# z in products of 512 columns, with its Silu placed anew and the background steps paced anew

## The chip, the cores and the metric

The kernel runs on one core of one Trainium2 chip. The metric is the device time of one execution in microseconds, as the median over runs.

## The reference

One decoder layer on 256 tokens of width 1024, in float32: a SwiGLU block, then a mixer with two branches side by side (a Mamba-2 branch, "ssd", and differential attention), then a second SwiGLU block, each with an RMS norm before and after it. The mixer multiplies its normed input `u` by one wide matrix and cuts the result in pieces:

```python
z, xbc, dt_raw, q, k, v, gate_logits = jnp.split(u @ w_in[l], IN_SPLITS, axis=-1)
...
y = y.reshape(b, L, SSD_D_INNER) * jax.nn.silu(z)
y = rmsnorm(y.reshape(b, L, SSD_GROUPS, SSD_D_INNER // SSD_GROUPS), 1.0).reshape(b, L, SSD_D_INNER) * norm_g
return y @ w_branch
...
gates = jax.nn.sigmoid(gate_logits + gate_b[l]).reshape(b, L, N_BRANCH, D_MODEL)
merged = gates[:, :, 0] * y_ssd + gates[:, :, 1] * y_att
```

z has 2048 columns. Its Silu gates the output of the ssd branch before that branch's group norm.

## The kernel before

**Products in split precision.** Each float32 operand is split in a high part and a low remainder that TensorE takes as float32r: a cast on ScalarE gives the high part (`whi`, L250), a subtraction on VectorE the low one (`wlo`, L253). A product is then the sum of three: high by high, high by low and low by high. `u` is kept with its high and low parts side by side (`[..., 0, :]` and `[..., 1, :]`), 256 tokens each.

**Two forms of such a product.** Both take a chunk of 1024 x 256 weights, as two halves of 128 output columns, with eight k-tiles each.
- `mm_t` (L294) writes 256 columns of one accumulator per half: per k-tile one product of `whi` with the high part of `u` (L301), one of `whi` with its low part (L302), and one of `wlo` with its high part (L304). One accumulator bank holds both halves, and one copy evicts it.
- `mm_w` (L306) multiplies `whi` with both parts of `u` at once, 512 columns (L316), and `wlo` with the high part, 256 columns (L315, L318). Each half has a bank of its own; the eviction is a copy of its second 256 columns on ScalarE (L320, or L323 with a scale) and an add of the first 256 on VectorE (L321, or L324).

Both take their accumulators from `pj`, three banks of PSUM; the other five are `bg`, for everything in the background.

**The order of the mixer.** Products of `u`: v, dt, B and C, then xs (eight chunks with `mm_w`), z (eight chunks with `mm_t`), q and k (four chunks each, with `mm_w`), the gates (L1375, `pgt`), then the ssd branch's output product (`pws`), the attention's (`pwd`) and the layer's. The last ones use `natural`, which takes half a token block at a time ("a call" below: 12 products of 512 columns).

**The background.** Between chunks `back.run(us)` hands out steps of generators in a queue. Each step yields a cost in microseconds written by hand; `run` adds its argument to a balance and takes steps until the balance is used up. A step that yields `BREAK` ends the run at hand and leaves the balance. The generators, in the order of the queue:
- `ssd_work`, per group of heads: two steps `X` (transposes `px`, L1061, and a product, 0.6 each), four steps `E` (1.4 each: small Relu and Exp on ScalarE, a clamp and a product with `cbm` on VectorE, from `acb`, which POOL's queue loads) and one with the products `py` (L1093, 1.6). They need the table with Exp.
- `ssd_norm`, per group, two under way at a time: 1.2 (the product with Silu(z), L1107, and a square), 1.5, a `BREAK`, 0.1 (the sum `pn`, L1119, and Ln and Exp) and 2.8 (the split to `yh`, `yl`).
- `att_work`: scores `psc` (L1166, L1167), softmax (2.3 a head), the turn `pa` (L1201), the combination (1.3 a head), `BREAK`, values `po` and a norm (1.8), the turn `pto` (L1240, 0.8), over pairs of heads.

The arguments are the constants `BG_US` (z), `QK_US` (q and k), `GATE_US` (gates) and `SSD_US` (`pws`, and the first half of `pwd`). `take()` hands out a chunk's weights and splits those three chunks ahead; the loads on SP's queue follow the splits.

**Who sets the order.** From the ends of the feed-forward blocks on, the planner of the framework orders each engine's instructions from their dependencies and their order in the code. After `own_order(PE)` (L1351), from the gates on, TensorE keeps the order of the code. `act_table(name)` loads a table of functions on ScalarE and ties itself behind all earlier `act()` calls and ahead of all later ones, so no Exp runs between the load of the Silu table (L1333) and the next load (L1336). Plain copies and casts aren't tied.

Of the kernel before, what the change touches and what calls it, by code (L numbers as in the profile page):

```python
# [18 lines left out]
AF = mybir.ActivationFunctionType  # L19
# [4 lines left out]
EXP_LN = "natural_log_exp_and_others"  # L24
# [3 lines left out]
T = 256  # L28
# [12 lines left out]
WARM = 3  # L41
FILL = 2
TAIL = 3
BG_US = 3.15
QK_US = 2.4
GATE_US = 1.75
SSD_US = 1.55
DOWN = {"f1": "p q1 p p q2 p ppp", "f2": "q1 p q2 p q3 ppp"}
FIRST, LAST = (1, 2, 3, 5, 7, 6, 4), (1, 6, 7, 2, 5, 3, 4)
BREAK, STOP = object(), object()  # L50
# [3 lines left out]
def tile_hybrid_layer(ctx: ExitStack, tc: tile.TileContext, x, ffn1_pre_g, ffn1_w_gate, ffn1_w_up,  # L54
# [4 lines left out]
    nc = tc.nc  # L59
# [5 lines left out]
    def k4(shape, name, dt=F32):  # L65
        return sb.tile(shape, dt, tag="k4", name=name, bufs=K4_BUFS)
# [4 lines left out]
    def k2(shape, name, dt=F32):  # L71
        return sb.tile(shape, dt, tag="k2", name=name, bufs=K2_BUFS)
# [7 lines left out]
    def pj(name):  # L80

        return ps.tile([P, 512], F32, tag="pj", name=name, bufs=3)

    def pjt(name):

        return pj(name).rearrange("p (m t) -> p m t", m=2)

    def bg(shape, name):
        return ps.tile(shape, F32, tag="bg", name=name, bufs=5)
# [169 lines left out]
    def split_to(n):  # L259

        while len(splits) < min(n, len(units)):
            of, p = units[len(splits)]
            if p is not None:
                splits.append(of.split(p))
                continue
            for _ in split_steps():
                pass

    def ahead_of(i, n):

        n *= 4
        while n > 0 and i < len(units):
            n -= 4 if units[i][1] is None else 1
            i += 1
        return i

    def take(ahead=AHEAD):

        i = taken[0]
        taken[0] += 1  # L280
        split_to(ahead_of(i, ahead))
        (of, p), w = units[i], splits[i]
        splits[i] = None
        if p is not None:
            return w
        his, los = w
        nj = chunks[of][1][1] // 2
        return (lambda j: his[j // nj][:, j % nj, :], lambda j: los[j // nj][:, j % nj, :])
# [5 lines left out]
    def mm_t(acc, w, act, k0=0, first=True, last=True, ks=range(KD)):  # L294

        (wh, wl), (ah, al, _) = w, act
        acc = acc if isinstance(acc, list) else [acc[:, m, :] for m in range(2)]
        for m in range(2):
            cs = slice(m * P, (m + 1) * P)
            for j in ks:  # L300
                nc.tensor.matmul(acc[m], wh(j)[:, cs], ah(k0 + j), start=first and j == ks[0], stop=False)  # L301
                nc.tensor.matmul(acc[m], wh(j)[:, cs], al(k0 + j), start=False, stop=False)  # L302
            for j in ks:
                nc.tensor.matmul(acc[m], wl(j)[:, cs], ah(k0 + j), start=False, stop=last and j == ks[-1])  # L304

    def mm_w(dst, name, w, act, scale=None):  # L306


        (wh, wl), (ah, _, ahl) = w, act
        for m in range(2):  # L310
            acc = pj(f"{name}{m}")
            cs = slice(m * P, (m + 1) * P)
            for j in range(KD):
                if j:
                    nc.tensor.matmul(acc[:, :T], wl(j)[:, cs], ah(j), start=False, stop=False)  # L315
                nc.tensor.matmul(acc, wh(j)[:, cs], ahl(j), start=j == 0, stop=j == KD - 1)  # L316
                if not j:
                    nc.tensor.matmul(acc[:, :T], wl(j)[:, cs], ah(j), start=False, stop=False)  # L318
            if scale is None:
                nc.scalar.copy(dst[:, m, :], acc[:, T:])  # L320
                nc.vector.tensor_tensor(dst[:, m, :], acc[:, :T], dst[:, m, :], ALU.add)  # L321
            else:
                nc.scalar.activation(dst[:, m, :], acc[:, T:], AF.Copy, scale=scale)  # L323
                nc.vector.scalar_tensor_tensor(dst[:, m, :], acc[:, :T], scale, dst[:, m, :], ALU.mult, ALU.add)  # L324

    def mm_nat(acc, w, act, k0, first, last, late):
# [25 lines left out]
    order = mybir.DependencyInfo(mybir.DependencyClass.NoSync, mybir.DependencyReason.DATA)  # L352

    def act_table(name):
        f = nc.scalar.preload_act_table_set(name)
        for prev in act_since:
            tc.add_manual_dep(f.ins, prev, order, reason="activation table")
        act_since.clear()
        act_fence[0] = f.ins.name

    def act(*args, **kw):
        a = nc.scalar.activation(*args, **kw)
        if act_fence[0] is not None:
            tc.add_manual_dep(a.ins, act_fence[0], order, reason="activation table")
        act_since.append(a.ins.name)
# [65 lines left out]
    def new_u(tag):  # L431
        for i in range(2):
            uT[i] = sb.tile([P, 4, 2, T], F32R, tag="u8", name=f"u{i}_{tag}", bufs=2)

    act_u = (lambda j: uT[j // 4][:, j % 4, 0, :], lambda j: uT[j // 4][:, j % 4, 1, :],
             lambda j: uT[j // 4][:, j % 4, :, :])
# [594 lines left out]
    for i in range(4):  # L1031
        acc = k2([P, 2, T], f"bc{i}")
        mm_w(acc, f"pbc{i}", take(), act_u)
        dst = (bT, cT)[i // 2]
        conv(acc, 16 + 2 * i, dst[:, (i % 2) * 2:(i % 2) * 2 + 2, :])
        if i == 1:
            cumulated()
# [13 lines left out]
    sz = [None] * 4  # L1051
# [52 lines left out]
    def ssd_norm(groups):  # L1104

        def one(g):
            nc.vector.tensor_tensor(xs[g], xs[g], sz[g], ALU.mult)  # L1107
            sq = k4([P, 4, T], f"sqy{g}")
            nc.scalar.activation(sq, xs[g], AF.Square)
            yield 1.2  # L1110
            nc.vector.tensor_tensor(sq[:, 0:2, :], sq[:, 0:2, :], sq[:, 2:4, :], ALU.add)
            nc.vector.tensor_tensor(sq[:, 0, :], sq[:, 0, :], sq[:, 1, :], ALU.add)
            ssum = k2([P, 2, T], f"ssum{g}", F32R)
            split(ssum[:, 0, :], ssum[:, 1, :], sq[:, 0, :])
            yield 1.5
            yield BREAK
            pn = bg([P, T], f"pn{g}")
            for i in range(2):
                nc.tensor.matmul(pn, ones_r, ssum[:, i, :], start=i == 0, stop=i == 1)  # L1119
            rs = sq[:, 1, :]  # L1120
            act(rs, pn, AF.Ln, scale=1.0 / 512, bias=eps_c)
            act(rs, rs, AF.Exp, scale=-0.5)
            yield 0.1
            for c in range(4):
                n = col["ng"] + g * 4 + c
                nc.vector.scalar_tensor_tensor(xs[g][:, c, :], xs[g][:, c, :], cols_a[:, n:n + 1], rs,
                                               ALU.mult, ALU.mult)
            yh[g] = k4([P, 4, T], f"yh{g}", F32R)
            yl[g] = k4([P, 4, T], f"yl{g}", F32R)
            split(yh[g], yl[g], xs[g])  # L1130
            xs[g] = sz[g] = None
            yield 2.8

        todo = [one(g) for g in groups]
        under_way = []
        while todo or under_way:
            if todo and len(under_way) < 2:
                under_way.append(todo.pop(0))
            for w in list(under_way):
                us = next(w, None)  # L1140
                if us is None:
                    under_way.remove(w)
                else:
                    yield us
# [170 lines left out]
    back = Background()  # L1315
    back.add(cb_work())
    for g in range(4):
        xs[g] = k4([P, 4, T], f"xs{g}")
        for i in range(2):
            acc = k2([P, 2, T], f"xr{g}{i}")  # L1320
# [5 lines left out]
    for g in range(4):  # L1326
        sz[g] = k4([P, 4, T], f"sz{g}")
        for i in range(2):
            acc = pjt(f"pz{g}{i}")
            mm_t(acc, take(), act_u)  # L1330
            nc.scalar.copy(sz[g][:, i * 2:i * 2 + 2, :], acc)
            back.run(BG_US)
    act_table(SILU)  # L1333
    for g in range(4):
        act(sz[g], sz[g], AF.Silu)
    act_table(EXP_LN)  # L1336
    back.add(ssd_norm(range(4)))
    for c in range(4):
        if c % 2 == 0:
            qT[c // 2] = k4([P, 4, T], f"q{c}")  # L1340
            kT[c // 2] = k4([P, 4, T], f"k{c}")
        o = (c % 2) * 2
        mm_w(qT[c // 2][:, o:o + 2, :], f"pq{c}", take(), act_u, 0.125)
        back.run(QK_US)
        mm_w(kT[c // 2][:, o:o + 2, :], f"pk{c}", take(), act_u)
        back.run(QK_US)

# [41 lines left out]
    for q in range(2):  # L1389
# [3 lines left out]

        natural(f"pws{q}", 4, lambda j: yh[j // 4][:, j % 4, :], lambda j: yl[j // 4][:, j % 4, :], gated, SSD_US)
    yh = yl = None
# [18 lines left out]
    for q in range(2):  # L1414
# [4 lines left out]
        def merge(b, acc):  # L1419
# [5 lines left out]
        natural(f"pwd{q}", 2, lambda j: oh[j // 4][:, j % 4, :], lambda j: ol[j // 4][:, j % 4, :], merge,  # L1425
                SSD_US if q == 0 else 0.0, (attended, lambda: turn_merged(2))[q])

    pg = load_gain(mix_post_g, "pg_mx")
    acc = [[bg([P, 512], f"acc_mx{b}{q}") for q in range(2)] for b in range(2)]
# [47 lines left out]
```

## Time and profile before

| what | value |
|---|---|
| median of 3 runs | 737.26 us (736.78 to 737.35) |
| profiled execution | 735.83 us |
| its span | 734.1 us |
| granted TensorE clock | 0.998 |
| TensorE busy | 724.9 us (99%) |
| VectorE busy | 598.8 us (82%) |
| ScalarE busy | 469.3 us (64%) |
| z products | 287.5 to 342.2 us of the span |
| q and k products | 342.2 to 394.3 us |

The span is what the trace covers; the execution is 1.7 us longer than it. Engines are PE (TensorE's matmuls), PEld (its weight loads), DVE (VectorE), ACT (ScalarE), POOL (GpSimd) and SP (SyncE). L316 is line 316 of the kernel, and `out<-in` are the kernel's names for the tiles.

### The profile page before, as it was taken

Reading aid. Unit: us, or ns where it says so; the run is one execution under the profiler, and the core shown is the slowest. Engines: PE = TensorE matmul, PEld = TensorE weight load, DVE = VectorE, ACT = ScalarE, POOL = GpSimd, SP = SyncE. Lnnn points to the kernel's source line nnn. Section 1 sums busy time; section 2 is a strip of 40 time slices with the busy share of each in tenths; the row PEclk is TensorE's granted clock in tenths of the full one; section 3 lists DMA queues with packets and bytes.
Section 4 is the critical chain, followed back from the end, with each engine's and each line's share of the span. In section 5 each row is a group of like instructions: output and inputs, shape, how many; then the busy total and the mean of one; then the engine's idle time right before and its main releaser. Section 6 shows DMA issues by size and latency. Waiting matters only on the chain.

```text
span 734.1 us, 10526 instructions
## 1 busy us (share of the span) xinstructions
PE 724.9 (99%) x4019; PEld 618.1 (84%) x4019; DVE 598.8 (82%) x928; ACT 469.3 (64%) x801; POOL 39.4 (5%) x72
## 2 busy tenths in 40 slices
PE   8999999999999999999999999999999999999996
PEld 7888888888878889999888788888888888888884
DVE  6978767998679999777996997784774878779994
ACT  6656556665567676869965577772663657566562
POOL 2800000000300000000000000000020000000000
PEclk9999999999999999999999999999999999999999
DMA  8874774369453657656564664374471764664541
GB/s 293 236 251 153 226 231 173 138 212 363 125 172 118 189 156 240 211 170 212 154 224 147 208 215 148 138 250 181 134 233 35 230 204 155 215 223 142 188 164 57
DMA packets 94210, 137.92 MB, mean 188 GB/s; under 512 B 2684, under 2 KB 68304, under 8 KB 94160
## 3 DMA queue, kind: packets, MB, share of 16 engines
q1 hardware_dynamic: 91488, 129.51, 53.8%
q0 software_dynamic: 2368, 7.22, 3.0%
q8 instruction: 31, 0.51, 0.3%
q10 hardware_dynamic: 304, 0.53, 0.2%
q14 instruction: 19, 0.16, 0.1%
HBM read 136.17 MB, written 1.08 MB: 187 GB/s over the span
## 4 chain that ended last, share of the span: by engine, by line
PE 97%; DVE 1%; issue 1%; DMA 1%; ACT 0%; DVEq 0%; SPq 0%
PE pup_f L316 9%; PE pg_f L316 9%; PE pgt L335 6%; PE pws L335 6%; PE acc_f1p L625 5%; PE acc_f2p L625 4%; PE pxs L316 4%; PE pg_f L315 4%; PE pup_f L315 4%; PE pn_f L345 3%; PE pn_f L335 3%; PE pn_mx L335 3%; PE acc_mx L573 3%; PE pwd L335 3%; PE acc_f1p L573 3%; PE pz L301 2%
## 5 line engine op out<-in xcount | busy, mean ns | idle before, releaser
L253 DVE TENSOR_TENSOR wlo<-raw,whi 128x1024 fp32r<-128x1024 f32 (+1 forms) x226 | 267.1, 1210 | 23.1 <-ACT whi L250 21.9
L250 ACT CAST whi<-raw 128x1024 fp32r<-128x1024 f32 (+1 forms) x225 | 226.8, 1045 | 18.0 <-DMA raw<-in_ffn_w_down_dram 4.2
L316 PE MATMUL pup_f<-u_f,whi 128*128 128x512 f32 x288 | 101.3, 396 | 0.0
L316 PE MATMUL pg_f<-u_f,whi 128*128 128x512 f32 x288 | 101.2, 396 | 0.0
L315 PE MATMUL pg_f<-u_f,wlo 128*128 128x256 f32 x252 | 70.6, 280 | 0.0
L315 PE MATMUL pup_f<-u_f,wlo 128*128 128x256 f32 x252 | 70.3, 279 | 0.0
L316 PEld LDWEIGHTS pup_f<-u_f,whi 128*128 128x128 f32 x288 | 52.8, 188 | 9.8
L316 PEld LDWEIGHTS pg_f<-u_f,whi 128*128 128x128 f32 x288 | 52.8, 188 | 9.7
L315 PEld LDWEIGHTS pg_f<-u_f,wlo 128*128 128x128 f32 x252 | 47.5, 188 | 1.8
L315 PEld LDWEIGHTS pup_f<-u_f,wlo 128*128 128x128 f32 x252 | 47.5, 189 | 1.6
L316 PE MATMUL pxs<-u_mx,whi 128*128 128x512 f32 x128 | 44.6, 397 | 0.0
L321 DVE TENSOR_TENSOR su_f<-pup_f,su_f 128x256 f32<-128x256 f32 x36 | 15.2, 422 | 26.1 <-ACT su_f L320 25.9
L320 ACT COPY su_f<-pup_f 128x256 f32<-128x256 f32 x36 | 13.4, 371 | 35.3 <-PE pup_f L316 35.2
L130 ACT CAST wqh<-wt 128x1024 fp32r<-128x1024 f32 x20 | 21.1, 1053 | 23.0 <-DVE wt L122 17.9
L335 PE MATMUL pgt<-whi,u_mx 128*128 128x512 f32 x128 | 33.1, 393 | 0.0
L301 PE MATMUL pz<-u_mx,whi 128*128 128x256 f32 x128 | 31.8, 285 | 0.0
L302 PE MATMUL pz<-u_mx,whi 128*128 128x256 f32 x128 | 31.4, 283 | 0.0
L315 PE MATMUL pxs<-u_mx,wlo 128*128 128x256 f32 x112 | 31.2, 279 | 0.0
L335 PEld LDWEIGHTS pgt<-whi,u_mx 128*128 128x128 f32 x128 | 23.6, 188 | 5.4 <-issue 0.7
L316 PEld LDWEIGHTS pxs<-u_mx,whi 128*128 128x128 f32 x128 | 23.2, 188 | 4.2
L291 ACT CAST gh_f<-sg_f 128x512 fp32r<-128x512 f32 x18 | 11.2, 621 | 21.6 <-DVE sg_f L771 21.6
L301 PEld LDWEIGHTS pz<-u_mx,whi 128*128 128x128 f32 x128 | 24.5, 191 | 0.2 <-issue 0.2
(401 smaller groups left out, 1679.7 us busy)
## 6 DMA issues: line engine op xcount, KB each, us to landing
raw<-in_w_in_dram SPq DMA_DIRECT2D x40, 1024.0 KB, 5.4
raw<-in_ffn_w_down_dram SPq DMA_DIRECT2D x22, 1024.0 KB, 4.9
raw<-in_ffn_w_gate_dram SPq DMA_DIRECT2D x20, 1024.0 KB, 5.8
raw<-in_ffn_w_up_dram SPq DMA_DIRECT2D x20, 1024.0 KB, 5.5
raw<-in_ssd_w_branch_dram SPq DMA_DIRECT2D x8, 1024.0 KB, 5.0
acb<-acd POOLq DMA_DIRECT2D x8, 512.0 KB, 5.3
raw<-in_da_w_branch_dram SPq DMA_DIRECT2D x4, 1024.0 KB, 5.1
raw<-in_w_out_dram SPq DMA_DIRECT2D x4, 1024.0 KB, 5.6
```

What stands on the lines that cost most here:

```text
L130: nc.scalar.copy(hi, src)
L250: copy(hi[:, js, :], r[:, q * nj + j:q * nj + j + n, :])
L253: nc.vector.tensor_sub(lo[:, js, :], r[:, q * nj + j:q * nj + j + n, :], hi[:, js, :].bitcast(F32))
L301: nc.tensor.matmul(acc[m], wh(j)[:, cs], ah(k0 + j), start=first and j == ks[0], stop=False)
L302: nc.tensor.matmul(acc[m], wh(j)[:, cs], al(k0 + j), start=False, stop=False)
L315: nc.tensor.matmul(acc[:, :T], wl(j)[:, cs], ah(j), start=False, stop=False)
L316: nc.tensor.matmul(acc, wh(j)[:, cs], ahl(j), start=j == 0, stop=j == KD - 1)
L321: nc.vector.tensor_tensor(dst[:, m, :], acc[:, :T], dst[:, m, :], ALU.add)
L335: nc.tensor.matmul(acc, a(k0 + j), b(j), start=first and i == 0, stop=last and i == 11)
L345: nc.tensor.matmul(accs[b], x_(k0 + j), w_(j), start=first and j == 0 and w_ is wh and x_ is acts[b][0], stop=last and j == 3 and w_ is wl)
L573: nc.tensor.matmul(acc[b][q], x_[:, ts], w_(kt)[:, halves[q]], start=begin and i == 0 and kt == 0 and x_ is ah and w_ is wh, stop=i == n - ...
L625: nc.tensor.matmul(bank[p], x_, w_, start=p not in begun, stop=last and p in (1, 5, 6, 7))
```

## The change

Four things change.
- z is made by `mm_w` like xs, q and k; each half's copy and add write `sz[g]` directly.
- The last background run of the z stage goes. The Silu of groups 0 and 1 comes right behind z's last chunk. The Silu of groups 2 and 3, the load of the Exp table, the queueing of `ssd_norm` and a run of `BG_US` follow q's first chunk; `mm_w` remembers its last scaled copy, and those two Silus are tied behind it on ScalarE.
- `BG_US` 3.15 to 2.7, `QK_US` 2.4 to 2.6, `SSD_US` 1.55 to 1.75.
- `act()` takes the instruction to be tied behind as an argument.

```diff
-BG_US = 3.15
-QK_US = 2.4
+BG_US = 2.7
+QK_US = 2.6
 GATE_US = 1.75
-SSD_US = 1.55
+SSD_US = 1.75
...
-                nc.scalar.activation(dst[:, m, :], acc[:, T:], AF.Copy, scale=scale)
+                last_copy[0] = nc.scalar.activation(dst[:, m, :], acc[:, T:], AF.Copy, scale=scale).ins
...
-    def act(*args, **kw):
+    def act(*args, behind=None, **kw):
         a = nc.scalar.activation(*args, **kw)
+        if behind is not None:
+            tc.add_manual_dep(a.ins, behind.name, order, reason="behind a copy")
...
     for g in range(4):
         sz[g] = k4([P, 4, T], f"sz{g}")
         for i in range(2):
-            acc = pjt(f"pz{g}{i}")
-            mm_t(acc, take(), act_u)
-            nc.scalar.copy(sz[g][:, i * 2:i * 2 + 2, :], acc)
-            back.run(BG_US)
+            mm_w(sz[g][:, i * 2:i * 2 + 2, :], f"pz{g}{i}", take(), act_u)
+            if (g, i) != (3, 1):
+                back.run(BG_US)
     act_table(SILU)
-    for g in range(4):
+    for g in (0, 1):
         act(sz[g], sz[g], AF.Silu)
-    act_table(EXP_LN)
-    back.add(ssd_norm(range(4)))
     for c in range(4):
...
         mm_w(qT[c // 2][:, o:o + 2, :], f"pq{c}", take(), act_u, 0.125)
+        if c == 0:
+
+            for g in (2, 3):
+                act(sz[g], sz[g], AF.Silu, behind=last_copy[0])
+            act_table(EXP_LN)
+            back.add(ssd_norm(range(4)))
+            back.run(BG_US)
         back.run(QK_US)
```

More of the change, by code (lines that the diff above doesn't have):

```diff
@@ L304, in mm_t @@
                 nc.tensor.matmul(acc[m], wl(j)[:, cs], ah(k0 + j), start=False, stop=last and j == ks[-1])
+    last_copy = [None]
     def mm_w(dst, name, w, act, scale=None):
```

## The prediction

> **What bounds the kernel now.** I read the page first (span and the chain that ended last), then the chain in order of time, then the groups of single tiles, the busy time by stretches, and the order in time on each engine around the z products.
>
> ```profile
> span 734.1 us, 10526 instructions
> ...
> PE 97%; DVE 1%; issue 1%; DMA 1%; ACT 0%; DVEq 0%; SPq 0%
> ```
>
> The chain of work that ended last is 97% TensorE. So a cover lost elsewhere costs only once it reaches TensorE, and a product made cheaper is worth its whole saving. What a product costs is not its duration, which overlaps the next one's, but the step from one start to the next. The chain in order of time gives it (start, length, what):
>
> ```profile
> 34.86 0.46 PE pg_f L316 x2
> ...
> 129.96 0.47 PE pup_f L316 x2
> ...
> 311.67 0.96 PE pz L304 x8
> ...
> 323.19 0.96 PE pz L304 x8
> ```
>
> The first two rows are 17 chunks apart, all made by `mm_w` (the form that z is to have): 95.10/17 = 5.594 us a chunk. The last two rows are four half chunks of z apart: 11.52/4 = 2.880, so 5.760 a chunk. Both forms stream the same columns: per k-tile three products of 256, or one of 512 and one of 256.
>
> ```profile
> L301 PE MATMUL pz<-u_mx,whi x128: 278/283/387, 287.7 to 341.0; 128*128 128x256 f32 x128
> ...
> L1331 ACT COPY sz<-pz x8: 566/586/589, 294.9 to 342.4; 128x512 f32<-128x512 f32 x8
> ```
>
> ```profile
> L320 ACT COPY xr<-pxs x16: 348/373/377, 243.5 to 288.2; 128x256 f32<-128x256 f32 x16
> L321 DVE TENSOR_TENSOR xr<-pxs,xr x16: 416/418/425, 244.1 to 288.6; 128x256 f32<-128x256 f32 x16
> ```
>
> **1. The products: -1.33 us.** L301 and L302 pair up 128 times over the eight chunks; each pair becomes one product, so 128 products go. By the chunk steps the saving is 8 x (5.760 - 5.594) = 1.33 us, 10 ns for each product that goes. All of it lies on TensorE's own path. The Trainium skill, "TensorE: Matmul & The Clock Gate", section "Back-to-back issue gap", gives an isolated step of N/2.4 + 2.5 ns, which would make this saving 2.5 ns x 128 = 0.32 us by estimate. The two steps in the rows above disagree with that by a factor of four, and I use the rows; by the page the sum below would come to +0.3 in place of -0.7.
>
> **2. The evictions.** A z chunk was evicted by one copy of 0.586. It now takes two copies of 0.373 and two VectorE adds of 0.418: ScalarE gets 8 x 0.160 = +1.3 us, VectorE 16 x 0.418 = +6.7. The three `pj` buffers now hold half a chunk each, so a buffer must be free 2 x 2.80 = 5.6 us after its last product, where z had 2 x 5.76 = 11.5 before. Whether there is room (columns: stretch, sum, then PE, PEld, DVE, ACT and so on):
>
> ```profile
> 238.00:287.50 49.50, 49.50 (x288) 43.41 (x287) 47.32 (x90) 34.74 (x59) 0.57 (x1) 1.00 0.59 181
> 287.50:342.20 54.70, 54.70 (x476) 52.89 (x475) 43.13 (x73) 41.08 (x84) 2.69 (x6) 1.00 0.66 203
> 342.20:394.30 52.10, 52.10 (x335) 44.44 (x334) 44.95 (x70) 39.23 (x71) 1.55 (x3) 1.00 0.66 212
> ```
>
> These are the xs, z, and q/k stretches. The costs that the background steps yield add up by hand: z handed out 8 x 3.15 = 25.2 and now 7 x 2.7 = 18.9; q and k 8 x 2.4 = 19.2 and now 2.7 + 8 x 2.6 = 23.5. So 6.3 us of steps leave z, 4.3 of them arrive in q/k, and 2.0 go on into the gates. Taking a yielded microsecond as one of VectorE, z stands at (43.13 + 6.7 - 6.3)/53.4 = 82% and q/k at (44.95 + 4.3)/52.1 = 95%. The xs stretch ran at 47.32/49.50 = 96% without TensorE pausing, so load alone should cost nothing: the splits of the weights, three chunks ahead, cover it. If that cover goes, the cost is the lag itself. What matters is bursts: part 3 and rival C.
>
> **3. The functions and the table.** The counts stay: four Silu calls, two table loads. Their order on ScalarE changes. Before, in the timeline of ScalarE:
>
> ```profile
> 344.69 1.28 ACT L355 ACT_TABLE_LOAD   x1
> 345.99 3.90 ACT L362 ACTIVATE sz<-sz 128x1024 f32<-128x1024 f32 x4
> 349.89 1.28 ACT L355 ACT_TABLE_LOAD   x1
> ...
> 354.58 0.37 ACT L320 COPY k<-pk 128x256 f32<-128x256 f32 x1
> 354.85 1.05 ACT L250 CAST whi<-raw 128x1024 fp32r<-128x1024 f32 x1
> 355.80 1.28 ACT L362 ACTIVATE E<-acb,acs 128x128 f32<-128x128 f32 x4
> 358.11 0.63 ACT L362 ACTIVATE E<-E 128x512 f32<-128x512 f32 x1 [1.03 <-DVE E L1078]
> ```
>
> ```profile
> L316 PE MATMUL pq<-u_mx,whi x64: 387/395/403, 342.2 to 387.9; 128*128 128x512 f32 x64
> ```
>
> ```profile
> 346.20 2.75 PE py L1093 x32
> ...
> 350.89 0.87 PE px L1061 x8
> ```
>
> Write T for the first q product, 342.2 now, 340.9 after. The second table load ended at T + 9.0. After the change q's second copy comes at T + 5.6, the last two Silus (1.95) and the load (1.28) end at T + 9.2: the window without Exp closes at the same place. What it covered has moved. Group 2's last three E steps and its `py` used to be handed out in z; by the sums of part 2 they now come in one handful behind the table load, at 3 x (1.28 + 0.63) = 5.7 us of ScalarE. The first half of k's first chunk ends at T + 8.4; its buffer is wanted again by q's second chunk, second half, at 5 x 2.80 = T + 14.0, or T + 14.9 with `px` in between. If ScalarE runs the three E first, the copy ends at T + 15.3 and the add of 0.42 at T + 15.7: a pause of 0.8 to 1.7. If not, none. Before, that buffer was wanted 2.75 later, because `py` ran in q. I take nothing: in the rows above the k copy at 354.58 ran ahead of an E step (355.80) that the code hands out earlier, so the planner does let evictions pass. The other end is rival A.
>
> **4. The gate stage and its bias.** Everything there comes one or two calls of `natural` later (a call is half a chunk). The new order makes the first `pn` about one q/k chunk (5.6) later, and the bias transfer `gb` waits for it:
>
> ```profile
> 388.57 0.53 POOL L1378 DMA_DIRECT2D gb<-in_gate_b_dram  x1 [38.24 <-PE pn L1119]
> ```
>
> ```profile
> gb<-in_gate_b_dram POOLq DMA_DIRECT2D x2, 512.0 KB, 4.2
> ```
>
> ```profile
> L1383 DVE TENSOR_TENSOR gt<-pgt,gb x8: 681/683/686, 406.3 to 444.0; 128x512 f32<-128x512 f32 x8
> ```
>
> Before it landed at 388.57 + 4.2 = 392.8, wanted at 406.3. Later by 5.6 it still has about 8 us. Cost nothing; without that room the gate's first accumulator would hold TensorE. POOL's queue holds nothing else there, and SP's transfers follow the splits, which keep their places.
>
> **5. SSD_US 1.75.** Adding up the yields call by call gives the old trace's places (`po` and `pto` in one call, `psc` of the last heads a call later). With the new numbers attention enters the gates a call later and has caught up by the seventh call of `pws`; from there to the end every step lies where it was. So the end loses and gains nothing, but at the seventh call the last `psc` comes right behind `po` and `pto`:
>
> ```profile
> 464.50 0.60 PE L1240 MATMUL pto<-ident,o 128*128 128x128 f32 x4
> ...
> 467.76 0.50 PE L1166 MATMUL psc<-k,q 64*128 64x128 f32 x4
> 468.08 0.61 PE L1167 MATMUL psc<-k,q 64*128 64x256 f32 x4
> 468.51 0.49 PE L1166 MATMUL psc<-k,q 64*128 64x128 f32 x4
> ```
>
> ```profile
> 465.93 0.74 DVE L1253 SCALAR_TENSOR_TENSOR ol<-pto,g,oh 128x512 fp32r<-128x512 f32 x1
> ```
>
> Four `psc` tiles, with `po` and `pto` still held, want six of five `bg` banks. The fourth waits for `pto`'s bank, which VectorE lets go at 465.93 + 0.74 = 466.67, 2.17 after `pto` began. It is due 0.35 (the four transposes, an estimate from their length) + 0.75 (467.76 to 468.51) + 0 to 0.43 (the step from 468.08 to 468.51) after that beginning: a pause of 0.6 to 1.1 us. Before, three rows of `pws` products between `pto` and 467.76 covered it. TensorE keeps the written order there, so all of `pws` is behind it. I take **+0.6**, the program-order end. Nothing is late next: the following `pa` is three calls off, as before.
>
> **Sum.** -1.33 + 0.6 = -0.7 us. The profiled execution took 735.83 (span 734.1 and 1.7 around it), so 735.1 by its measure; the median of the runs is 737.26, 1.43 above it, so **736.5**.
>
> **The rivals.**
> A, slower: k's first eviction is late (part 3). Beside the three E, two weight CASTs of 1.05 can stand ahead of the copy: ScalarE is free at T + 9.2 + 5.7 + 2.1 = T + 17.0, the add ends at T + 17.8 against T + 14.9, a pause of 2.9 to 3.8, say 3.2. Total -0.7 + 3.2 = +2.5: 739.8. It decides from 2.2 us of pause on, where the sum passes +1.47. For it: the code hands the E out ahead of k's casts and copies, and they are ready once the table is loaded. Against: the k copy of 354.58. Chance 0.25.
> B, nothing pauses, neither in q nor at `psc` (a bank comes free sooner): -1.33, 735.9. Chance 0.26.
> C, the z ring: bursts of E in the first chunks, in the timeline of ScalarE:
>
> ```profile
> 301.12 0.62 ACT L362 ACTIVATE E<-E 128x512 f32<-128x512 f32 x1
> ```
>
> The first z product started at 287.7 (row of L301), so with 2.80 a half and 0.9 for a `px` z's second chunk has its first half done near 297.0, and its buffer is wanted 5.6 later, at 302.6. ScalarE is in E until 301.7, so copy and add end at 302.5, or about 1 us later if VectorE's product of the same E goes first. Price up to 0.9: -0.7 + 0.9 = +0.2, 737.5. Chance 0.14.
> D, the change doesn't do what it says: columns alone set the pace, a product of 512 takes two steps of 0.120, and there is nothing to save. Then +0.6, 737.9. The 17 chunks above speak against it. Chance 0.05.
> The forecast itself keeps 0.30.
>
> **How the numbers follow.** 0.2% is 1.47 us, about what a measurement of this kernel can tell from no change. The three runs shown lie between 736.78 and 737.35, so I give each case a scatter of 0.3. Case B lies at -1.33, just inside the bound, so some four in ten of it fall beyond (0.10), and one in six of the forecast (0.05): faster 0.15. Slower is nearly all of A and a few of C and D: 0.26. The rest, 0.59, is within. The range runs from case B less the scatter, 735.5, to 739.4, inside case A, whose pause may be shorter: it leaves out some 0.08 below and 0.12 above.
>
> **What would show it.** L301 to L304 without rows; `pz` under L315, L316 and L318, 16 halves 2.80 apart; 128 records of TensorE fewer. Twice as many adds for z under L321. The last table load ending about 9 us behind the first q product, and the first k copy ahead of group 2's last E (forecast) or behind it (A, with a gap in TensorE some 15 us behind the first q product). At the last `psc` a gap of 0.6 to 1.1 and no `pws` between it and `pto`. `pto` and the first `pwd` in the same order as before. The prediction is wrong if z's halves are not 2.80 apart, or TensorE pauses in a place not named here.

## The result, and the profile after

The changed kernel takes **742.77 us** (median of six runs, 742.48 to 743.59) against 737.31 for the kernel before (six runs beside them, 736.78 to 738.89): ratio **1.0078, 95% interval 1.0068 to 1.0088**. It is slower by 5.5 us; the prediction was 736.5 with a range that ended at 739.4. The profiled execution took 743.22 us. Of all runs in this document one, of e10 below, was slow with 2348.59 us, and the ratios leave it out.

The page of the changed kernel, its span and its chain by engine:

```profile
span 741.3 us, 10291 instructions
...
PE 87%; DVE 7%; ACT 3%; issue 2%; DMA 1%; DVEq 0%; SPq 0%; ACTq 0%
```

The chain was 97% TensorE; now 10% of it runs over VectorE and ScalarE. The waits of TensorE say where (line that waited, releaser: total, times, longest):

```profile
PE psc L1170 <- DVE ol L1257: 1.9, 1, 1.9
...
PE py L1097 <- DVE E L1087: 1.4, 1, 1.4
...
PE pq L318 <- DVE k L323: 0.5, 1, 0.5
```

None of these three stands in the profile before. To see what each stretch gained or lost, I take the first starts of the tiles that open them, in the changed kernel

```profile
L318 PE MATMUL pz<-u_mx,whi x128: 391/395/504, 289.6 to 342.6; 128*128 128x512 f32 x128
...
L318 PE MATMUL pq<-u_mx,whi x64: 391/395/496, 342.9 to 390.8; 128*128 128x512 f32 x64
...
L337 PE MATMUL pgt<-whi,u_mx x128: 387/389/504, 396.8 to 445.5; 128*128 128x512 f32 x128
...
L337 PE MATMUL pwd<-whi,oh x16: 389/389/476, 506.5 to 520.9; 128*128 128x512 f32 x16
```

and in the kernel before (its `pz` and `pq` rows stand in the prediction):

```profile
L335 PE MATMUL pgt<-whi,u_mx x128: 387/389/504, 394.2 to 442.7; 128*128 128x512 f32 x128
...
L335 PE MATMUL pwd<-whi,oh x16: 389/389/476, 499.4 to 513.8; 128*128 128x512 f32 x16
```

| stretch | before | after | difference |
|---|---|---|---|
| z (first `pz` to first `pq`) | 54.5 | 53.3 | -1.2 |
| q and k (to first `pgt`) | 52.0 | 53.9 | +1.9 |
| gates and `pws` (to first `pwd`) | 105.2 | 109.7 | +4.5 |
| sum | 211.7 | 216.9 | +5.2 |

The sum agrees with the medians (+5.5). The two profiled executions differ by more, 7.2 us of span, because the changed one also reached z 1.9 later, in code that the change doesn't touch (last section). So I compare all kernels by these stretches, and their times only by medians.

**q and k.** ScalarE of the changed kernel in order of time:

```profile
350.93 1.28 ACT L357 ACT_TABLE_LOAD   x1
352.23 1.28 ACT L364 ACTIVATE E<-acb,acs 128x128 f32<-128x128 f32 x4
...
357.32 1.03 ACT L250 CAST whi<-raw 128x1024 fp32r<-128x1024 f32 x1
358.25 0.37 ACT L325 ACTIVATE q<-pq 128x256 f32<-128x256 f32 x1
358.53 0.62 ACT L322 COPY k<-pk 128x256 f32<-128x256 f32 x2
```

From 352.23 to 357.32 stand three E steps of group 2 back to back, 1.7 each. The first k copy comes at 358.53, 15.6 behind the first q product (342.9), with a cast and a copy of q ahead of it too. On TensorE the group's products `py`, which stand between the two halves of q's second chunk, waited for the last E (second row of the waits above).

The third row of the waits is another place, 31 us behind the first q product: a bank of q's third chunk waited for the eviction of k's second chunk. On ScalarE that eviction stood behind three E steps again, those of group 3 (365.44 to 370.5), and a cast:

```profile
371.47 0.62 ACT L322 COPY k<-pk 128x256 f32<-128x256 f32 x2
```

```profile
373.97 0.50 PE L318 MATMUL pq<-u_mx,whi 128*128 128x512 f32 x1 [0.47 <-DVE k L323]
```

What a pause costs is again read from the steps of TensorE. The step ahead of `py` is 356.63 to 358.46 = 1.8, where it is 0.3 in the kernel before: 1.5 lost. The step ahead of 373.97 is 0.9, where a product of 512 columns steps by 0.24: 0.6 lost. Together that is 2.1. The stretch shows 0.2 less, because a pair of `pn` products of 0.24, the second that ran inside it in the kernel before (393.93, just ahead of the first gates product), now runs in the gates stretch.

**The last scores.** TensorE around the last `psc`:

```profile
470.08 0.60 PE L1244 MATMUL pto<-ident,o 128*128 128x128 f32 x4
...
471.37 0.38 PE L1170 MATMUL psc<-k,q 64*128 64x128 f32 x2
471.60 0.59 PE L1171 MATMUL psc<-k,q 64*128 64x256 f32 x2
474.06 0.48 PE L1170 MATMUL psc<-k,q 64*128 64x128 f32 x2 [1.87 <-DVE ol L1257]
...
474.90 1.22 PE L337 MATMUL pws<-whi,yh 128*128 128x512 f32 x4
475.92 1.91 PE L337 MATMUL pws<-wlo,yh 128*128 128x512 f32 x4
477.63 1.86 PE L337 MATMUL pws<-whi,yl 128*128 128x512 f32 x4
479.33 1.09 PE L337 MATMUL pws<-whi,yh 128*128 128x512 f32 x4
```

The fourth `psc` waits for `pto`'s bank, as forecast, but for much longer. The step at 471.60 is 2.46, where two such products take 0.22 (four take 0.43, 468.08 to 468.51, in the prediction's rows): a pause of 2.2. The view of the waits says 1.9 because the record of a product is longer than its step.

The wait also parts the score products. In the kernel before, the last eight run in two rows of four, from 468.51 (in the prediction) to the next `pws`:

```profile
469.37 1.21 PE L335 MATMUL pws<-whi,yh 128*128 128x512 f32 x4
```

That is 0.86. Here they run in four rows of two, 471.37 to 474.90 = 3.53, which is 2.7 more: the pause of 2.2 and 0.4 for the rows of two.

Why the pause is so long stands on VectorE:

```profile
468.65 3.50 DVE L253 TENSOR_TENSOR wlo<-raw,whi 128x1024 fp32r<-128x1024 f32 x3 [6.61 <-ACT whi L250]
...
473.26 0.74 DVE L1257 SCALAR_TENSOR_TENSOR ol<-pto,g,oh 128x512 fp32r<-128x512 f32 x1
```

and the reason for three splits at once on ScalarE:

```profile
466.28 1.28 ACT L357 ACT_TABLE_LOAD   x1
467.57 2.94 ACT L250 CAST whi<-raw 128x1024 fp32r<-128x1024 f32 x3
```

The bank is let go at 473.26 + 0.74 = 474.00, 3.9 after `pto` began, not 2.17. VectorE had first waited 6.61 for casts that stood behind the gates' Sigmoid and its table loads, and then had three splits (3.50), a product for the gates and a reduction to do before the eviction.

The TensorE rows above show a second loss. Rows of four `pws` products normally step by 0.91; those at 475.92 and 477.63 step by 1.7. The busy times by stretches (sum, then PE, PEld, DVE, ACT, POOL, then the granted clock):

```profile
476.00:478.00 2.00, 2.00 (x6) 1.58 (x5) 1.59 (x4) 0.97 (x6) 0.00 (x0) 0.50 0.53 202
478.00:480.00 2.00, 2.00 (x7) 1.56 (x6) 0.47 (x1) 1.89 (x5) 0.00 (x0) 0.67 0.01 5
```

The granted clock falls to a half for some 3.4 us behind the pause: eight products from 475.92 to 479.33 took 3.41 where two steps of 0.91 take 1.82, so **1.6 us** more. `PEclk` in the page's 40 slices still reads 9 everywhere; windows of 2 us show it.

The theory to test: +5.2 = -1.2 (the products) + 2.1 (three E steps in a row ahead of `py` and of k's eviction) + 2.7 (the `psc` pause and the rows of two) + 1.6 (the clock behind it). The `pn` pair only moves 0.24 from one stretch to the next.

### The profile page after: what moved, and what is told of

Its sections match the earlier page's. It is cut to its first block, busy times and chain, and to the rows that moved or that the text cites. A ratio compares the mean times of both kernels' runs of the same rounds, so it can differ in the third digit from the quotient of the medians.

```text
span 741.3 us, 10291 instructions
## 1 busy us (share of the span) xinstructions
PE 728.1 (98%) x3891; PEld 613.6 (83%) x3891; DVE 603.3 (81%) x944; ACT 469.7 (63%) x809; POOL 39.5 (5%) x72
## 4 chain that ended last, share of the span: by engine, by line
PE 87%; DVE 7%; ACT 3%; issue 2%; DMA 1%; DVEq 0%; SPq 0%; ACTq 0%
PE pg_f L318 9%; PE pup_f L318 9%; PE pgt L337 6%; PE acc_f1p L629 5%; PE pz L318 4%; PE pg_f L317 4%; PE pxs L318 4%; PE pup_f L317 4%; PE pws L337 4%; PE pn_f L347 3%; PE pn_f L337 3%; PE pn_mx L337 3%; PE acc_mx L577 3%; PE pwd L337 3%; PE acc_f1p L577 3%; DVE wlo L253 2%
## 5 line engine op out<-in xcount | busy, mean ns | idle before, releaser
L318 PE MATMUL pz<-u_mx,whi 128*128 128x512 f32 x128 | 44.8, 398 | 0.0
L130 ACT CAST wqh<-wt 128x1024 fp32r<-128x1024 f32 x20 | 21.1, 1053 | 23.5 <-DVE wt L122 23.5
L317 PE MATMUL pz<-u_mx,wlo 128*128 128x256 f32 x112 | 31.3, 280 | 0.0
L337 PEld LDWEIGHTS pgt<-whi,u_mx 128*128 128x128 f32 x128 | 23.5, 188 | 5.3 <-issue 0.3
```

Source lines behind the costliest of these rows:

```text
L130: nc.scalar.copy(hi, src)
L337: nc.tensor.matmul(acc, a(k0 + j), b(j), start=first and i == 0, stop=last and i == 11)
```

## The experiments

Stretches of all kernels, by first starts as above:

| kernel | z | q and k | gates and `pws` | sum | median us | ratio to before (95%) |
|---|---|---|---|---|---|---|
| before | 54.5 | 52.0 | 105.2 | 211.7 | 737.31 | |
| changed | 53.3 | 53.9 | 109.7 | 216.9 | 742.77 | 1.0078 (1.0068 to 1.0088) |
| e1_ssd180 | 53.2 | 54.0 | 105.5 | 212.7 | 738.28 | 1.0012 (0.9997 to 1.0026) |
| e2_before_ssd165 | 54.5 | 52.0 | 106.2 | 212.7 | 738.85 | 1.0018 (1.0005 to 1.0031) |
| e3_z_only | 53.9 | 52.0 | 105.2 | 211.1 | 737.10 | 0.9988 (0.9975 to 1.0002) |
| e4_run_in_z | 53.3 | 54.6 | 109.6 | 217.5 | 743.62 | 1.0069 (1.0048 to 1.0091) |
| e5_fill | 53.2 | 54.0 | 108.1 | 215.3 | 740.40 | 1.0055 (1.0041 to 1.0068) |
| e6_silu_old_place | 53.3 | 57.6 | 105.4 | 216.3 | 743.02 | 1.0087 (1.0069 to 1.0105) |
| e7_silu_new_place | 53.9 | 56.2 | 105.2 | 215.3 | 739.90 | 1.0056 (1.0034 to 1.0078) |
| e8_best | 53.1 | 54.2 | 105.2 | 212.5 | 738.02 | 1.0017 (1.0006 to 1.0027) |
| e9_z_rebalanced | 53.2 | 54.1 | 105.2 | 212.5 | 737.64 | 1.0014 (1.0005 to 1.0023) |
| e10_e_steps_later | 53.3 | 51.6 | 105.5 | 210.4 | 736.34 | 0.9987 (0.9973 to 1.0001) |

Each ratio is to runs of the kernel before on the same chip (their medians: 737.12 for e1 to e4, 736.63 for e5 to e8, 736.78 for e9 and e10). The stretches do not always give the whole difference: in e6 the sum is 4.6 longer and the median 6.4, and its one profile reached z 2.0 later than that of the kernel before.

### The scores one call away from `pto`

```diff
 # the changed kernel
-SSD_US = 1.75
+SSD_US = 1.8
```

> The changed kernel with SSD_US 1.80 in place of 1.75. Added up by hand, this alone puts the last psc one call (2.7 us of pws products) behind po and pto. Theory: the pause of 2.2 us before its second half and the 1.6 us of half clock behind it both go, so 742.8 falls by 3.5 to 4.4, to 738.4 to 739.3, and the clock row of that stretch is 1.00. Rival 1 (the bank is late whatever the order, because ScalarE and VectorE are late there): the pause moves to the next bg tile, the time stays within 1 us of 742.8. Rival 2 (the half clock has a cause of its own, not the pause): only 2.2 us go, 740.6.

The theory held (738.28, just below its 738.4 to 739.3): +1.2 us against before instead of the changed kernel's +5.5; the gates stretch is back at 105.5, where 0.24 over the kernel before is the `pn` pair. TensorE:

```profile
466.68 0.60 PE L1244 MATMUL pto<-ident,o 128*128 128x128 f32 x4
467.03 1.16 PE L337 MATMUL pws<-whi,yh 128*128 128x512 f32 x4
...
469.94 0.50 PE L1170 MATMUL psc<-k,q 64*128 64x128 f32 x4
```

Twelve products stand between `pto` and the scores again, and none of TensorE's waits is at `psc`. One constant, 0.05 larger, is worth 4.3 us: four fifths of the change's loss was its `SSD_US`. The loss in q and k (54.0) stays, as it should.

### The same neighbourhood in the kernel before

```diff
 # the kernel before
-SSD_US = 1.55
+SSD_US = 1.65
```

> The kernel before with SSD_US 1.65 in place of 1.55 and nothing else. Added up by hand, this alone puts po, pto and the last psc in one call. Theory: the same pause appears in the old kernel, 0.6 us if VectorE takes pto's eviction at once, up to 2.2 if splits stand ahead of it, and 1.6 more if the clock follows: 738 to 741.7 against 737.3. Rival (the denser pace by itself costs nothing and the loss came from the new z stage): 737.3 within 0.5.

Here too the last `psc` comes right behind `pto`, and the pause is small. TensorE, then VectorE:

```profile
466.10 0.60 PE L1240 MATMUL pto<-ident,o 128*128 128x128 f32 x4
...
467.61 0.59 PE L1167 MATMUL psc<-k,q 64*128 64x256 f32 x2
468.33 0.48 PE L1166 MATMUL psc<-k,q 64*128 64x128 f32 x2
...
469.18 1.19 PE L335 MATMUL pws<-whi,yh 128*128 128x512 f32 x4
```

```profile
463.82 2.36 DVE L253 TENSOR_TENSOR wlo<-raw,whi 128x1024 fp32r<-128x1024 f32 x2 [6.68 <-ACT whi L250]
...
467.54 0.74 DVE L1253 SCALAR_TENSOR_TENSOR ol<-pto,g,oh 128x512 fp32r<-128x512 f32 x1
```

Two splits, done by 466.2, before `pto`'s eviction can begin: the bank is free 2.2 after `pto` began, the prediction's 2.17. The step ahead of the fourth tile is 467.61 to 468.33 = 0.72 where 0.22 is usual, a pause of 0.5. From `pto` to the next `pws` are 3.08, against 470.08 to 474.90 = 4.82 in the changed kernel. The clock doesn't fall here: the products behind step by 0.91. The prediction's price for the pause was right for VectorE as it stood in the trace of before, and wrong for VectorE as the change left it. It had nothing for the rows of two, which stand here too: the stretch is 1.0 longer (106.2 against 105.2), 0.5 for the pause and 0.4 for them, and the median 1.7 longer.

### The pause filled with products

```diff
 # the changed kernel: eight products of 512 columns more, whose result nothing reads
-            for head in here:
+            for i, head in enumerate(here):
+                if n == 3 and i == 1:
+                    pf = pj("fill")
+                    for _ in range(8):
+                        nc.tensor.matmul(pf, yh[0][:, 0, :P], yh[0][:, 0:2, :], start=True, stop=True)
```

> The changed kernel with eight products of 512 columns into the idle third pj bank ahead of the second head of the last psc, where TensorE waited 1.9 us for pto's bank. They compute nothing that is used. Theory (the pause itself makes the clock fall to half): the eight take 1.8 us of the wait, the clock row behind it stays 1.00, and 1.6 us come back: 742.8 - 1.6 = 741.2, with the last psc ending at the same distance from po. Rival (the half clock there is chance, or comes from the small products of po, pto and psc ahead of it): clock still 0.5 to 0.7, time 742.8 to 743.

TensorE and the busy times:

```profile
467.75 0.60 PE L1244 MATMUL pto<-ident,o 128*128 128x128 f32 x4
...
469.14 2.09 PE L1273 MATMUL fill<-yh 128*128 128x512 f32 x8
...
472.57 1.20 PE L337 MATMUL pws<-whi,yh 128*128 128x512 f32 x4
```

```profile
474.00:476.00 2.00, 2.00 (x10) 1.65 (x10) 2.00 (x4) 1.25 (x6) 0.00 (x0) 1.00 0.40 155
```

From `pto` to `pws` it is 467.75 to 472.57 = 4.82, exactly as without the extra products, so the bank's wait is the same; but TensorE is busy in it, the clock stays at 1.00, and the stretch is 1.6 shorter (108.1 against 109.7). The small products of `po`, `pto` and `psc` are there as before, so the fall of the clock follows from TensorE's pause and not from them, and it is worth 1.6. What is left over e1 is 108.1 - 105.5 = 2.6: the pause of 2.2, and the 0.4 for the rows of two, which stand here too.

### z's products alone

```diff
 # the kernel before
-            acc = pjt(f"pz{g}{i}")
-            mm_t(acc, take(), act_u)
-            nc.scalar.copy(sz[g][:, i * 2:i * 2 + 2, :], acc)
+            mm_w(sz[g][:, i * 2:i * 2 + 2, :], f"pz{g}{i}", take(), act_u)
```

> The kernel before with z made by the form with products of 512 columns and nothing else: old paces, old place of the Silus. Theory: z's products are worth -1.3 us and the old py cover in q is still there: 736.0 against 737.3. Rival (the extra 6.7 us of VectorE adds make splits or evictions late in z): the z stretch is not shorter than the old one, and the time is 737.5 or more.

z is 0.6 shorter, not 1.2: one pause, of the kind of rival C (an E burst ahead of a z eviction), in a later chunk than C had it and inside its price of up to 0.9:

```profile
323.79 0.50 PE L316 MATMUL pz<-u_mx,whi 128*128 128x512 f32 x1 [0.40 <-DVE sz L321]
```

q and k are untouched at 52.0. So the products are worth what part 1 said, and with the old order hardly a new wait arises; the interval (0.9975 to 1.0002) just takes in no change. The smaller `BG_US` of the changed kernel removes this pause (z 53.3); e7 below, with the old one, has it again.

### The run back in z

```diff
 # the changed kernel
-            if (g, i) != (3, 1):
-                back.run(BG_US)
+            back.run(BG_US)
 ...
             back.add(ssd_norm(range(4)))
-            back.run(BG_US)
```

> The changed kernel with its run of BG_US put back behind z's last chunk and taken out of q's first chunk; the Silus stay as changed. Theory: the three E steps of group 2 run ahead of the Silu table, so py no longer waits 1.4 us for them, nor q's later half 0.5 us for k's eviction: 742.8 - 1.9 = 740.9, with the pause at the last psc unchanged. Rival (the E steps push the Silu table back by their 5.7 us of ScalarE, and q's evictions behind it): a pause of the same size moves to q's or k's accumulators, 742.8 within 0.7.

The rival was right in its mechanism; 743.62 is just above its bound of 743.5. With the run behind z's last chunk, E steps come ahead of the Silu table, and the second table load ends at T + 11.3 (T is the first q product) where the changed kernel's ended at 350.93 + 1.28 = 352.21, T + 9.3. Waits of TensorE:

```profile
PE pq L318 <- DVE k L323: 1.2, 1, 1.2
PE pk L318 <- DVE q L326: 1.1, 1, 1.1
```

q and k take 54.6, 0.7 more than in the changed kernel. `py` no longer waits, but the eviction of q's first chunk is late in its place (1.1), and the wait for the eviction of k's second chunk, behind the E steps of group 3, has grown from 0.5 to 1.2. So E steps cost ahead of the table load as well as behind it.

### The Silus and the paces, apart

The kernel before with z's products, the new paces (2.7, 2.6) and a `SSD_US` of 1.8, all four Silus in the old place:

```diff
 # the kernel before, with mm_w for z
-BG_US = 3.15
-QK_US = 2.4
+BG_US = 2.7
+QK_US = 2.6
 ...
-SSD_US = 1.55
+SSD_US = 1.8
```

> The changed kernel's z and its paces, SSD_US 1.80, but the four Silus and both table loads behind z's eighth run as before the change. Theory: only one E step of group 2 (not three) and py are left for q, so the q/k stretch (first q product to first gate product) is 52 to 52.6 us, against 53.9 with the Silus moved and 52.0 before; z 53.4; no pause at psc. Time 738.3 (SSD_US 1.80 with the Silus moved) - 1.5 = 736.8. Rival (what moved the loss into q is the smaller handful of the pace, not the Silus): q/k stays 53.5 or more and the time 738.3.

And the changed kernel with the old paces, its Silus in the new place:

```diff
 # the changed kernel
-BG_US = 2.7
-QK_US = 2.6
+BG_US = 3.15
+QK_US = 2.4
 ...
-SSD_US = 1.75
+SSD_US = 1.55
```

> The reverse: z by the new form and the Silus in the new place, but the old paces 3.15, 2.4 and 1.55. One E step and py are behind the table load. Theory: q/k 52.0 to 53.0 by the one E step, no pause at psc, z 53.4 to 53.9: 736.5 to 737.5 against 737.1 before. Rival (the new place of the Silus by itself costs q/k its 1.9 us whatever the pace): q/k 53.9, time 738.3.

Waits of TensorE, of the first and of the second:

```profile
PE pk L316 <- DVE q L324: 4.0, 1, 4.0
```

```profile
PE pq L318 <- DVE k L323: 2.5, 1, 2.5
```

Behind both waits the clock fell, as behind the `psc` pause (columns as above; e6, then e7):

```profile
356.00:358.00 2.00, 2.00 (x8) 1.13 (x9) 1.82 (x2) 2.00 (x4) 0.00 (x0) 0.50 0.80 191
```

```profile
364.00:366.00 2.00, 2.00 (x9) 1.73 (x8) 2.00 (x5) 2.00 (x8) 0.00 (x0) 0.56 1.02 353
```

The waits take 4.2 and 2.7 by the steps of TensorE (351.15 to 355.56 and 359.18 to 362.07, less 0.24 each). Of what q and k lost against the kernel before, the `pn` pair allowed for, that leaves about 1.6 in each case, the price of the clock in e5.

My theory that moving the Silus was the cause fell. e6's rival, the smaller pace, has the stretch right (53.5 or more) and the time far too small (738.3; measured 743.02); in e7 theory and rival are both too small (739.90). With the new paces the old place costs 57.6 in q and k, the new one 53.9: given the smaller `BG_US`, the new place is the better by 3.7, of which 1.6 is the clock. As I read the traces, E steps that come next to the table switch cost, wherever it is: in e6 the second table load ends at T + 9.9, and `py`, which in the kernel before ran inside q's first chunk and gave its evictions time, comes only at 357.19, behind the wait. No run takes the two apart. With the old paces the new place isn't good either (56.2), and for another reason, on ScalarE:

```profile
359.61 0.38 ACT L325 ACTIVATE q<-pq 128x256 f32<-128x256 f32 x1 [4.88 <-PE pq L318]
```

ScalarE stood idle for 4.88 us waiting for a q product, with k's copies, 359.89, behind it in its order though k's products had run from 347.3 to 352.8: there the order of the copies, not ScalarE's load, held the bank.

### Two tries to mend z's pause

From e3, with paces between the old and the new ones:

```diff
 # the kernel before, with mm_w for z
-BG_US = 3.15
-QK_US = 2.4
+BG_US = 3.05
+QK_US = 2.5
```

> A version to beat both: z by the new form, Silus in the old place, BG_US 3.05, QK_US 2.5, SSD_US 1.55. Added up by hand no run of z hands out more than two E steps (three with 3.15, behind which z's eviction was 0.4 us late), py of group 2 is handed out in z, and attention falls where it fell before the change. Theory: z 53.2 to 53.4, q/k 52.0, the rest as before: 737.1 - 1.2 = 735.9. Rival (z keeps a pause of about half a microsecond wherever the bursts lie): 736.5.

From e3, with the old paces and 0.8 of work moved from behind z's fourth chunk to behind its fifth:

```diff
 # the kernel before, with mm_w for z
-            back.run(BG_US)
+            back.run(BG_US + {(1, 1): -0.8, (2, 0): 0.8}.get((g, i), 0.0))
```

> The kernel before with z by the new form, the old paces and the old place of the Silus, and one thing more: 0.8 of BG_US goes from the run behind z's fourth chunk to the run behind its fifth, so that the fourth hands out two E steps and not three. Theory: z's one pause (0.4 us, its eviction behind four E on ScalarE in a row) goes, py of group 2 still runs inside the Silus' window in q, and nothing else moves: z 53.2 us, q/k 52.0, 737.1 - 0.4 = 736.7 or the same step below its own runs of before, 1.2 in all. Rival (with z 0.4 shorter and ScalarE's work the same, the Silus stand later against q's products, and a pause of 0.5 to 1 comes in q, as in the version with 3.05 and 2.5): q/k 52.5 to 53, no gain over the version without the shift.

Both took z's pause away (53.1, 53.2) and paid 2.1 for it in q and k, in the same two waits (`pk` for q's eviction, 1.6 together). ScalarE of e9:

```profile
349.18 1.28 ACT L355 ACT_TABLE_LOAD   x1
...
352.38 0.64 ACT L323 ACTIVATE q<-pq 128x256 f32<-128x256 f32 x2
```

In e8 and e9 q's first copy starts 11.3 behind the first q product (341.1 in e9), and TensorE waits for it. In the kernel before (352.14 - 342.2 = 9.9) and in e3 (351.81 - 341.7 = 10.1) it doesn't. Of the 1.2 between e3 and e9, 0.7 is the shorter z, which lets the first q product come earlier, and the rest is ScalarE, which reaches the table load later. So the saving in z came back as a wait in q: the old order kept half of its 1.2 in e3, and none where z had all of it. e8's theory and its rival both missed (738.02, ratio 1.0017); of e9's two, the rival had the wait, at 0.5 to 1 where it was 2.1.

### The E steps later

e1, with no steps behind q's first chunk, where the table is switched, and 2.7 + 8 x 2.6 = 23.5 spread over the seven places behind it:

```diff
 # the changed kernel
-SSD_US = 1.75
+SSD_US = 1.8
 ...
             back.add(ssd_norm(range(4)))
-            back.run(BG_US)
-        back.run(QK_US)
+        else:
+            back.run(3.36)
         mm_w(kT[c // 2][:, o:o + 2, :], f"pk{c}", take(), act_u)
-        back.run(QK_US)
+        back.run(3.36)
```

> The changed kernel with SSD_US 1.80 whose q and k runs are dealt anew: none behind q's first chunk, 3.36 behind each of the seven that follow, the same sum. So k's first evictions are no longer behind three E steps on ScalarE. Theory (that handful is what TensorE waits for in q): k's first copy comes within 4 us of the table load, TensorE goes on with q's second chunk, py finds its E ready, the 1.4 us wait for E and the 0.5 us wait for k both go: q/k 52.0 to 52.6, 738.3 - 1.5 = 736.8. Rival (ScalarE is behind by the whole Silu window and only the place of the pause changes): q/k 53.5 to 54.5 with one or two pauses on q's or k's accumulators, 738.3 or more.

ScalarE:

```profile
350.43 1.28 ACT L357 ACT_TABLE_LOAD   x1
...
352.68 0.40 ACT L364 ACTIVATE E<-acb,acs 128x128 f32<-128x128 f32 x1
352.98 0.35 ACT L322 COPY k<-pk 128x256 f32<-128x256 f32 x1
...
353.83 0.36 ACT L322 COPY k<-pk 128x256 f32<-128x256 f32 x1
```

k's two copies now come 1.3 and 2.1 behind the table load, in the middle of an E step, and q and k have no pause (51.6). The theory held, with a little to spare (736.34; it said 736.8). `py` has moved too, from 358.46 to 361.69, and the E steps of group 3 no longer stand three in a row ahead of a k copy; the run doesn't say what each of these is worth. From the first z product to the first `pwd` it takes 210.4: 6.5 less than the changed kernel and 1.3 less than the kernel before, which is what part 1 said the products save (the `pn` pair shifts 0.24 from q and k to the gates here too). In time it is 736.34 against 736.78, ratio 0.9987 (0.9973 to 1.0001): likely a gain of about 0.1%, but the interval just reaches no change. It is the best version found, and by its stretches the only one that keeps the whole saving.

## Why the prediction was wrong, point by point

- **Part 1, the products (-1.33).** Right: z gave -1.2 in the changed kernel, and the whole -1.3 was kept in e10. TensorE has 3891 records where it had 4019, the 128 fewer that were forecast.
- **Part 2, evictions and load.** Right that load alone costs nothing; q and k with 23.5 us of steps in them ran without a pause in e10. The bursts decided, as the part said. The shares of VectorE were off: forecast 82% in z and 95% in q and k, measured 45.7/53.3 = 86% and 46.5/54.0 = 86%. A yielded microsecond is not one of VectorE.
- **Part 3, "I take nothing".** This step failed, by +2.1. Its times were nearly right: the table load was forecast to end at T + 9.2 and ended at T + 9.3; the three E took 5.1 where it added up 5.7; k's first copy, with E first, was to end at T + 15.3 and began at T + 15.6, behind a cast and a copy of q that the sum left out. Its choice between the two ends was wrong. I chose by one k copy in the trace of before that ran ahead of an E step; here three E were handed out ahead of k's first copies, and ScalarE ran all three first. With none handed out there (e10) the copies came through. So E stood ahead of the copy, as rival A said, but the losses fell elsewhere than A had them: 1.5 where `py` waited for the last E, and 0.6 where q's third chunk waited for k's second, behind the next three E. Neither place was named, and by its own last sentence the prediction is wrong on that count too.
- **Part 4, the gates' bias.** Right: `pgt` never waited for `gb`.
- **Part 5, "I take +0.6".** The place and the mechanism were right (the fourth `psc` for `pto`'s bank, no `pws` between), the size wrong: 2.2 for the pause. The step that failed is the 2.17 until the bank is free, read off a VectorE that was idle ahead of that eviction. The text itself said that attention enters the gates a call later, and so moves against the Sigmoid and the casts behind it; I did not ask what would then be queued on VectorE. Three splits were: 3.9. The part also had nothing for the score products running in rows of two: 0.4.
- **Missing: the clock.** No part asked what a pause does beyond its own length. Behind 1.9 us of waiting the granted clock was 0.50 and 0.67: +1.6 (e5).
- **Sum.** Forecast -0.7; measured -1.2 + 2.1 + 2.7 + 1.6 = +5.2. The range ended at 739.4 because A was priced with part 5 at 0.6. With both failing together and the clock, it was 3.4 short.
- **Still open.** Why the planner put one k copy ahead of E in the kernel before: e10 shows that what is handed out where matters, not the planner's rule. And how the loss of e6 divides between the late table load and the missing `py`.

## What to carry to other kernels

Price a wait for a buffer by the queue of the engine that frees it, as that queue will stand after the change: the same wait was 0.5 us with VectorE done with its splits (e2) and 2.2 with three splits still ahead. When steps are paced by hand, look for handfuls that stand in front of evictions, next to a table switch above all: in e10, with nothing handed out at the switch and the rest dealt evenly, no wait was left. And when TensorE bounds, a pause of about 2 us should be priced with the clock behind it, which here cost 1.6 more each time.

## What the runs showed of the hardware

**The clock behind a pause.** After the 1.9 us wait, with 3.4 us of small products ahead of it (`po`, `pto`, `psc`, from 468.75 on), the granted clock was a half from about 475.9 to 479.3, for 1.6 us of loss; with products in the gap it was 1.00. The same wait in e4 and the waits of 2.5 (e7) and 4.0 (e6) were each followed by a half clock of 3.4 us as well; ahead of the one in e6 stood 8 us of q and k products and nothing small. Waits of 0.5 (e2), 0.9 (e8, e9), 1.1 and 1.2 (e4) and 1.4 (q, changed kernel) were not: the clock stayed at 1.00. These are single profiles, so they give no limit. The half clock need not begin with the wait: in the changed kernel it set in 1.9 us behind the wait's end (474.06), in e7 0.3 behind it, in e6 just ahead of it. The Trainium skill, "TensorE: Matmul & The Clock Gate", section "Part 1: The HAM clock gate (the "warmup" mystery)", says that the array goes to half clock after at least one idle window of about 3.4 us, and that the window runs freely. The half clock and its length, 3.4 us, agree, and a window of its own would fit the different places where it sets in. The idle time that brought it on was shorter than that window in three of four cases (1.9 twice, 2.5), and whether 1.9 us would do so on every phase of the window no run shows.

**The start.** Kernels with the same code up to z reach it up to 2.5 us apart (287.3 in e5, 289.7 in e4 and e6). The first products `pn_f` show where it begins: the same eight products take 3.75 us in the changed kernel, from 7.31 on, and 2.53 in the kernel before, from 6.73 on. The granted clock reads 1.00 in both, so the traces don't say why. So part of a single run's scatter is set in its first microseconds, and says nothing of a change further on.
